# Decode products on GpSimd, whole-head state runs, paired readout transposes and earlier loads for a mean

## The chip, the core and the metric

The kernel runs on one core of a Trainium2 chip. The core has a matrix engine (TensorE, in the profile PE, with its weight loads as PEld), a vector engine (VectorE, DVE), a scalar engine (ScalarE, ACT), a general engine (GpSimd, POOL) and a queue processor (SyncE, SP) that issues most transfers between the chip's memory and the on-chip buffers. Matrix products land in banks of a small accumulator memory (PSUM), and another engine must read them out before a bank can be used again. The metric is the device time of one execution in microseconds; the time before is the median of 3 runs.

## What is computed

One inference step of a two-layer decoder, at once for a prompt of 1024 tokens and for 8 decode sequences with one new token each. The first layer mixes tokens by gated linear attention with 4 heads (key width 96, value width 192), in parallel with attention into 256 memory tokens; the second by windowed attention. Each layer ends in an MLP with a squared ReLU, and every part has a norm before and after it. The part of the decode step that matters here is, for each sequence b and head h,

```
S_new[b,h] = exp(g[b,h])[:, None] * S[b,h] + k[b,h][:, None] * v[b,h][None, :]     # 96 x 192
o[b,h]     = q[b,h] @ S_new[b,h]                                                   # 192
```

`S_new` is an output, and `o` goes, normed and multiplied with a gate silu(r), into the output projection `w_out` of the layer together with the 1024 prompt tokens.

## The kernel before, in words

All activations are kept transposed, features on the 128 partitions and tokens along the free axis, in three chunks of 384, 384 and 264 columns; the last one has the 8 decode columns at its end. Products in 32-bit precision are built of three passes (high x high, high x low, low x high), so a 128 x 384 output tile of a projection with 1024 inputs is 8 x 3 = 24 matrix steps. A float tile is split into its high part by a cast on ScalarE (L158) and its low part by a subtraction on VectorE (L159).

The order of the work on each engine is made by a planner: each instruction has a priority, by its place in the code unless `high_priority` lifts it, and the planner takes for each engine the first one that its cost model holds to be ready. The order is then fixed, and at run time each engine works through its list in order and waits where it must. Transfers on SP go in order too. Buffers come from rings (`bufs=2` means two).

The stage of the change is the end of the first layer's mixer. `r_units` (from L1525) computes the gate for row tiles 3, 4, 5 of each chunk: nine units, chunk by chunk, each one projection and a chain of elementwise steps (L1542 to L1549) whose result goes to a scratch tensor `srd` (L1550). The loop over the nine units (L2001) steps the decode generator `gla_dec` after every second unit. For each head h that generator loads the state `sin` (96 partitions, 8 sequences x 192; L1951) and the values `vb`, broadcast to all 96 partitions from a scratch tensor `vdd` (L1953), and then, for each of the 8 sequences, ScalarE scales the state (L1957) and VectorE adds key times value to it (L1958). The state is stored (L1959). `readout` multiplies queries and states (L1965), 8 products of 32 rows, and copies the result (L1967); the readout of a head is issued when the next head has been, and that of the last head at the end, before the norm of the heads.

`make_o0` makes the input of the output projection for one chunk, in six row tiles: it loads the gate from `srd` (L1985, two buffers), transposes up to three blocks of tokens on TensorE into a bank (L1988, two banks; L1990 for the decode columns of the last chunk), multiplies bank and gate on VectorE (L1992) and splits the result. Chunk 0 is made after the sixth gate unit. `out_proj` then runs eight output tiles per chunk (`part`); chunk 1 is made after three output tiles of chunk 0 and chunk 2 after three more.

In `mlp` the up-projection runs over pairs of output tiles, seven products each in the order `ORDER`; `product` ends in `evict` (L722 for the first product, L724 to L736). `square_mean` loads a chunk of the residual in four parts (L813, two buffers), squares them on ScalarE (L187), adds the squares on VectorE (L194) and forms their mean on TensorE. It is called for pairs 2, 3 and 4 at the fourth product (L998).

Of the kernel before, what the change touches and what calls it, by code (L numbers as in the profile page):

```python
# [8 lines left out]
F32 = mybir.dt.float32  # L9
# [7 lines left out]
P = 128  # L17
D = 1024
KT = 8
# [30 lines left out]
def hybrid_decoder_step(ctx: ExitStack, tc: tile.TileContext, A, O):  # L50
# [31 lines left out]
    srd = dram.tile([P, 6, NT], F32, tag="srd", name="srd")  # L82
    mkd = dram.tile([2, P, 2, MEM], F32, tag="mkd", name="mkd")
    wfd = dram.tile([12, P, KT, P], F32, tag="wfd", name="wfd")
    vdd = dram.tile([NDEC, 768], F32, tag="vdd", name="vdd")
    mvd = dram.tile([2, P, 2, MEM], F32, tag="mvd", name="mvd")
    apd = dram.tile([2, P, NPL, 2, HALF], F32, tag="apd", name="apd")
    awd = dram.tile([2, 7, NJ, P, 2, HALF], F32, tag="awd", name="awd")
# [545 lines left out]
                h = 2 * hp + j  # L634
                nc.vector.tensor_copy(by_group(dq[rows, hp, :]), otv[rows, hp, :, h : h + 5 : 4])

    def out_proj(l, make_o, src_pool, st, ff, xsrc, psum=True, oh0=None):
        wO = st.enter_context(tc.tile_pool(name=nm("wO"), bufs=5, reuse_waits="tile"))
        f0 = ff.pools[0]
        if psum:  # L640
            set_extra(st.enter_context(tc.tile_pool(name=nm("pmo"), bufs=2, space=PSUM, reuse_waits="tile")), 2)
        W = [wload(wA if m < 3 else wO, A["w_out"][l, m]) for m in range(KT)]
        OH, FT = {}, {}

        def prep(c):
            if c == 0 and oh0:
                OH[c] = oh0
                return
            OH[c] = xtiles(c)
            make_o(c, OH[c])  # L650

        R = {}

        def part(c, ms, pool):
            n = CH[c][1]
            if c not in FT:
                FT[c] = pool.tile([P, KT, n], F32, tag="f", name=nm("f"))
                R[c] = Residual(c, FT[c], G_MIXPOST + l, xsrc[c], G_FFNPRE + l)
            for m in ms:
                ps = mmps()  # L660
                proj(ps, W[m], OH[c], n)
                with first():
                    nc.scalar.copy(FT[c][:, m, :], ps[:, :n])
                R[c].feed(m)

        prep(0)
        part(0, range(0, 3), f0)
        prep(1)
        part(0, range(3, 6), f0)
        prep(2)  # L670
        part(0, range(6, 8), f0)
        src_pool.close()
        f2 = ff.open("right")
        f1 = ff.open("rest")
        xsp[0] = ff.rest.enter_context(tc.tile_pool(name=nm("xs"), bufs=2, side="right", reuse_waits="tile"))
        unit = 3 * KT * 384
        res = [R[0].finish(1.3 * unit)]
        part(1, range(KT), f1)
        res.append(R[1].finish(1.3 * unit))
        part(2, range(KT), f2)  # L680
        res.append(R[2].finish(1.3 * unit))
        set_extra(None, 0)
        ff.f = [FT[c] for c in range(3)]
        return res
# [74 lines left out]
    def mlp(l, X, ff):  # L759
# [48 lines left out]
        def square_mean(c):  # L808
            c0, n = CH[c]
            st = Stats(n, "sx")  # L810
            for j in range(4):
                xs = tmp3([P, 2, n])
                nc.sync.dma_start(xs, xd[c][:, 2 * j : 2 * j + 2, :])  # L813
                st.add(xs)
            v = st.mean(X[c][1], 8 * 3 * 4 * SUB)
            nc.scalar.activation(X[c][1], v, AF.Square, scale=math.sqrt(EPS * D / P))

        K1, K2 = slice(0, 4), slice(4, 8)
        pieces = [
# [159 lines left out]
        for t, (j, i) in enumerate(items):  # L979
            if i == ORDER[0]:  # L980
                if j == 0:
                    tiles = [tp.tile([P, 768], F32, tag=tag, name=nm("c")) for tag in ("t3", "t3", "tq", "tq")]
                    rows = [x[:, :HALF] for x in tiles]
                else:
                    tiles = [ff.pools[j % 2].tile([P, 4, HALF], F32, tag="f", name=nm("aw"))]
                    rows = [tiles[0][:, q] for q in range(4)]
            if xsteps:
                next(xsteps.pop(0))
                if xsteps:
                    next(xsteps.pop(0))  # L990
            prepare(t + (3 if j == 0 else 5))
            product(j, i, rows)
            if i == ORDER[0] and pend is not None:
                factors(*pend[2:])
                store(*pend)
                pend = None
            if i == ORDER[3] and 2 <= j < 5:
                square_mean(j - 2)  # L998
            if i == ORDER[-1]:
                more = w4.tile([P, 3, HALF], F32, tag="w4", name=nm("am"))  # L1000
                pend = (j, tiles, rows, more)
# [382 lines left out]
    with ExitStack() as sl0:  # L1384
# [10 lines left out]
        with ExitStack() as sla:  # L1395
# [349 lines left out]
            with ExitStack() as sg:  # L1745
# [139 lines left out]

                def after_first():
                    pend()
                    nc.sync.dma_start(vdd[:, :384], vrow)
                gp = sg.enter_context(tc.tile_pool(name="glb", bufs=2, reuse_waits="tile"))
                S = gp.tile([DK, H, DV], F32, tag="S", name="S", bufs=1)  # L1890

# [38 lines left out]
                for i in range(NB):  # L1930
                    if i == 4:
                        pend()
                        nc.sync.dma_start(vdd[:, 384:], vrow)
                    gla_block(1, i)
                in_r([2])
                nc.sync.dma_start(O["sg_prompt"].rearrange("h k v -> k h v"), S)
# [7 lines left out]
        def gla_dec(dp, d1):  # L1944
            qmk = d1.tile([DK, H, NDEC, 32], F32, tag="qmk", name="qmk")
            nc.gpsimd.memset(qmk, 0.0)
            last = None
            for h in range(H):
                hv = slice(h * DV, h * DV + DV)
                sin = dp.tile([DK, NDEC, DV], F32, tag="sin", name=nm("sin"))  # L1950
                nc.sync.dma_start(sin, A["state_gla"][:, h].rearrange("b k v -> k b v"))  # L1951
                vb = dp.tile([DK, NDEC, DV], F32, tag="vb", name=nm("vb"))
                nc.sync.dma_start(vb, vdd[:, hv].unsqueeze(0).to_broadcast([DK, NDEC, DV]))  # L1953
                for e in range(2):
                    nc.vector.tensor_copy(qmk[:, h, e::2, e], qd[:DK, QIDX[h], e::2])
                for bb in range(NDEC):
                    nc.scalar.mul(sin[:, bb, :], sin[:, bb, :], eg[:, h * NDEC + bb : h * NDEC + bb + 1])  # L1957
                    STT(sin[:, bb, :], vb[:, bb, :], qd[:DK, KIDX[h], bb : bb + 1], sin[:, bb, :], ALU.mult, ALU.add)  # L1958
                nc.sync.dma_start(O["sg_sample"][:, h].rearrange("b k v -> k b v"), sin)  # L1959
                def readout(h=h, hv=hv, sin=sin):  # L1960
                    ops = stps()
                    row = Row()
                    for e in range(2):
                        for g in range(4):
                            row(nc.tensor.matmul(ops[32 * g : 32 * g + 32, :DV], qmk[:, h, 2 * g + e, :],  # L1965
                                                 sin[:, 2 * g + e, :], start=(e == 0), stop=(e == 1)))
                    nc.vector.tensor_copy(vdec[:, hv], ops[:, :DV])  # L1967

                if last:
                    last()  # L1970
                last = readout
                yield
            last()
            head_norm(vdec, [vdec[:, h * DV : h * DV + DV] for h in range(H)], P, d1)

        ff = Sums()
        with ExitStack() as so:
            srp = so.enter_context(tc.tile_pool(name="srp", bufs=2, reuse_waits="tile"))

            def make_o0(c, ohl):  # L1980
                c0, n = CH[c]
                oh, ol = ohl
                for m in range(6):
# [7 lines left out]
                                         ident.rearrange("p (g c) -> p g c", c=32)[:, :, :2], start=True, stop=True)  # L1991
                    TT(sr, tps[:, :n], sr, ALU.mult)  # L1992
                    split(oh[:, m, :], ol[:, m, :], sr)
                split(oh[:, 6:8, :], ol[:, 6:8, :], qm[:, :, c0 : c0 + n])

            with ExitStack() as sd:
                dp = sd.enter_context(tc.tile_pool(name="gdec", bufs=2, side="right", reuse_waits="tile"))
                d1 = sd.enter_context(tc.tile_pool(name="gdec1", bufs=1, side="right", reuse_waits="tile"))
                gt = sd.enter_context(tc.tile_pool(name="gt", bufs=2, reuse_waits="tile"))
                dec = gla_dec(dp, d1)  # L2000
                for u, _ in enumerate(r_units([3, 4, 5], pool=gt)):  # L2001
                    if u % 2 == 0:
                        next(dec, None)
                    if u == 5:
                        oh0 = xtiles(0)
                        make_o0(0, oh0)
            X = out_proj(0, make_o0, svp, so, ff, [A[f"xT{c}"] for c in range(3)], False, oh0)
        pmd.close()

# [477 lines left out]
def _arrays(inp):  # L2487
# [46 lines left out]
    wg[:, 1:17] = inp["w_gate_up"][0]  # L2534
    wg[0, 0] = inp["b_gate"][0]
    a["wg"] = wg.reshape(GR, 2, 192)
    a["state_gla"] = np.ascontiguousarray(inp["state_gla"][0])
    mk = inp["cache_mem_k"].reshape(2, NDEC, MEM, 2, P)
    a["mem_kT"] = np.ascontiguousarray(mk.transpose(0, 1, 4, 3, 2))
    a["mem_v"] = np.ascontiguousarray(  # L2540
# [28 lines left out]
def hp_list(hp):  # L2569
# [2 lines left out]


_OUT = {
    "yT": (P, KT, NT), "sg_prompt": (H, DK, DV), "sg_sample": (NDEC, H, DK, DV),
    "swa_kp": (P, 2, WIN), "swa_vp": (P, 2, WIN), "swa_ks": (NDEC, WIN, 256), "swa_vs": (NDEC, WIN, 256),
    "mem_k": (2, P, 2, MEM), "mem_v": (2, P, 2, MEM),
}
# [2 lines left out]
def _unpack(o):  # L2581
# [3 lines left out]
    sp = [np.ascontiguousarray(o[k].transpose(2, 1, 0)).reshape(1, WIN, 4, 64) for k in ("swa_kp", "swa_vp")]  # L2585
    return (
        np.ascontiguousarray(y[:SEQ])[None], np.ascontiguousarray(y[SEQ:])[:, None],
        o["sg_prompt"][None, None], o["sg_sample"][None], sp[0], sp[1],
        o["swa_ks"].reshape(NDEC, WIN, 4, 64), o["swa_vs"].reshape(NDEC, WIN, 4, 64), mem[0], mem[1],
    )  # L2590

# [16 lines left out]
```

## Time and profile before

| what | value |
|---|---|
| median of 3 runs | 2121.37 us (2118.39 to 2122.22) |
| the profiled execution: time / span | 2120.73 us / 2118.9 us |
| TensorE busy | 2098.3 us, 99% |
| VectorE busy | 1537.3 us, 73% |
| ScalarE busy | 1104.3 us, 52% |
| GpSimd busy | 116.6 us, 6% |
| granted TensorE clock | 1.0 |

The span runs from the first to the last instruction of the profiled execution. An engine's time is busy while it executes an instruction; matrix steps overlap, so that a step's own duration (0.33 us for 128x384) is longer than the distance to the next one. A row of a timeline gives start, duration, engine, line, operation, output<-inputs and shapes, and in brackets how long the engine stood idle before and which instruction ended that. A row of waits gives who waited for whom, us in total, how often, and the longest.

### The profile page before, as it was taken

The numbers are of one execution on the slowest core, as the hardware profiler recorded it, in microseconds if no ns is written. First come the engines' busy times: TensorE is split into PE (matmuls) and PEld (weight loads), VectorE is DVE, ScalarE is ACT, GpSimd is POOL, SyncE is SP. The second block draws the span as 40 slices with busy tenths as digits, with TensorE's granted clock in tenths as the row PEclk, the third lists the DMA queues.
The fourth block names the chain that finished last, engine by engine and source line by source line (L and its number), as shares of the span: only waits on it lengthen the run. The fifth ranks groups of instructions, "written<-read, shape, count | busy, mean of one in ns | idle before, by whom it ended". The sixth has DMA issues, their size and how long they took to land.

```text
span 2118.9 us, 41850 instructions
## 1 busy us (share of the span) xinstructions
PE 2098.3 (99%) x16870; PEld 2026.3 (96%) x16870; DVE 1537.3 (73%) x2869; ACT 1104.3 (52%) x2211; POOL 116.6 (6%) x176
## 2 busy tenths in 40 slices
PE   8999999999999999999999999999999999999998
PEld 6979999899999999999999988899999999999998
DVE  7657648669887777855788457677987777865767
ACT  6365536457645444333555256676664454433454
POOL 0012000000000000034200002000000000000010
PEclk9999999999999999999999999999999999999999
DMA  5521117443654459667444304425454437935345
GB/s 174 168 85 43 41 51 193 151 143 121 193 166 131 145 165 318 224 221 250 161 126 137 104 22 142 158 96 175 140 189 162 163 115 257 314 103 170 101 130 151
DMA packets 143768, 323.22 MB, mean 153 GB/s; under 512 B 16153, under 2 KB 58321, under 8 KB 143217
## 3 DMA queue, kind: packets, MB, share of 16 engines
q1 hardware_dynamic: 125712, 275.20, 40.5%
q0 software_dynamic: 8816, 32.47, 4.6%
q10 hardware_dynamic: 9040, 12.82, 1.6%
q8 instruction: 134, 2.20, 0.4%
q14 instruction: 66, 0.54, 0.1%
HBM read 227.78 MB, written 93.74 MB: 152 GB/s over the span
## 4 chain that ended last, share of the span: by engine, by line
PE 90%; DVE 5%; DMA 3%; ACT 2%; issue 1%; SPq 0%; DVEq 0%; ACTq 0%
PE mm L268 10%; PE mm L280 7%; PE mx L268 7%; PE mx L903 6%; PE mx L905 5%; PE mx L904 5%; PE mx L1148 5%; PE mx L1149 5%; PE mx L1150 5%; PE mm L903 3%; PE mm L905 3%; PE mm L904 3%; PE mm L1148 2%; PE mm L1149 2%; PE mm L1150 2%; PE kv L268 2%
## 5 line engine op out<-in xcount | busy, mean ns | idle before, releaser
L158 ACT CAST wh<-ws 128x512 fp32r<-128x512 f32 (+1 forms) x271 | 199.5, 737 | 302.1 <-PE mx L904 96.8
L903 PE MATMUL mx<-xf,wh 128*128 128x258 f32 x1048 | 297.2, 284 | 0.8 <-DVE aw L732 0.8
L905 PE MATMUL mx<-xf,wl 128*128 128x258 f32 x1048 | 295.7, 282 | 0.0
L904 PE MATMUL mx<-xf,wh 128*128 128x258 f32 x1048 | 295.5, 282 | 0.0
L159 DVE TENSOR_TENSOR wl<-ws,wh 128x512 fp32r<-128x512 f32 (+1 forms) x271 | 226.0, 835 | 54.5 <-ACT wh L158 48.5
L158 ACT CAST wh<-wr 128x1024 fp32r<-128x1024 f32 x102 | 106.9, 1048 | 280.8 <-PE sx L1149 265.3
L1148 PE MATMUL mx<-sa,wh 128*128 128x258 f32 x840 | 237.4, 283 | 0.0
L1149 PE MATMUL mx<-sa,wh 128*128 128x258 f32 x840 | 235.9, 281 | 0.0
L1150 PE MATMUL mx<-sa,wl 128*128 128x258 f32 x840 | 235.9, 281 | 0.0
L159 DVE TENSOR_TENSOR wl<-wr,wh 128x1024 fp32r<-128x1024 f32 x102 | 126.2, 1237 | 139.7 <-ACT wh L158 139.2
L903 PEld LDWEIGHTS mx<-xf,wh 128*128 128x128 f32 x1048 | 197.6, 189 | 1.6 <-ACT aw L943 1.0
L904 PEld LDWEIGHTS mx<-xf,wh 128*128 128x128 f32 x1048 | 198.0, 189 | 0.4
L905 PEld LDWEIGHTS mx<-xf,wl 128*128 128x128 f32 x1048 | 197.8, 189 | 0.0
L1148 PEld LDWEIGHTS mx<-sa,wh 128*128 128x128 f32 x840 | 159.0, 189 | 0.1
L1149 PEld LDWEIGHTS mx<-sa,wh 128*128 128x128 f32 x840 | 158.7, 189 | 0.1
L1150 PEld LDWEIGHTS mx<-sa,wl 128*128 128x128 f32 x840 | 158.3, 188 | 0.0
L268 PE MATMUL mm<-xh,wh 128*128 128x384 f32 (+1 forms) x480 | 155.2, 323 | 0.0
L159 DVE TENSOR_TENSOR sa<-ra,sa 128x1032 fp32r<-128x1032 f32 (+1 forms) x128 | 140.7, 1099 | 20.0 <-ACT sa L158 19.6
L268 PE MATMUL mm<-xh,wl 128*128 128x384 f32 (+1 forms) x480 | 152.4, 317 | 0.0
L268 PE MATMUL mm<-xl,wh 128*128 128x384 f32 (+1 forms) x480 | 152.3, 317 | 0.0
L158 ACT CAST sa<-ra 128x1032 fp32r<-128x1032 f32 (+1 forms) x128 | 120.9, 945 | 52.2 <-PE sf L1150 23.5
L903 PE MATMUL mm<-xf,wh 128*128 128x258 f32 x520 | 147.3, 283 | 0.0
(602 smaller groups left out, 6194.2 us busy)
## 6 DMA issues: line engine op xcount, KB each, us to landing
ra<-awd SPq DMA_DIRECT2D x92, 516.0 KB, 4.4
ws<-in_w_up SPq DMA_DIRECT2D x64, 512.0 KB, 6.3
wr<-in_w_downb SPq DMA_DIRECT2D x64, 512.0 KB, 6.0
awd<-aw SPq DMA_DIRECT2D x26, 1032.0 KB, 7.6
awd<-am SPq DMA_DIRECT2D x28, 774.0 KB, 8.5
ws<-in_w_out SPq DMA_DIRECT2D x26, 512.0 KB, 3.8
ws<-in_w_in_a SPq DMA_DIRECT2D x20, 512.0 KB, 3.8
ws<-wfd SPq DMA_DIRECT2D x15, 512.0 KB, 3.8
```

The lines of the kernel that those rows point to most:

```text
L158: nc.scalar.copy(hi, src)
L159: (eng or nc.vector).tensor_tensor(lo, src, f32(hi), ALU.subtract)
L268: mm = nc.tensor.matmul(ps[:M, :n], w_[:, k, :M], x_[:, k, :], start=(i == 0), stop=(i == 3 * KT - 1))
L280: nc.tensor.matmul(ps[:, :n], w_[:, k, :], x_[:, k, :], start=(k == 0 and t == 0), stop=(k == KT - 1 and t == 2))
L903: nc.tensor.matmul(ps, wh(k), xh, start=(k == 0), stop=False)
L904: nc.tensor.matmul(ps, wh(k), xl, start=False, stop=False)
L905: mm = nc.tensor.matmul(ps, wl(k), xh, start=False, stop=(k == n - 1))
L1148: nc.tensor.matmul(ps, wh[:, q, ms], h, start=(jj == 0 and q == 0), stop=False)
L1149: nc.tensor.matmul(ps, wh[:, q, ms], lo, start=False, stop=False)
L1150: mm = nc.tensor.matmul(ps, wl[:, q, ms], h, start=False, stop=end)
```

## The change

Three places are edited.

In `gla_dec`, GpSimd multiplies keys and values of all eight sequences of a head in one operation, in place in `vb`; ScalarE scales the state as before, and VectorE adds the products four sequences at a time. The state input and output and the scratch tensor `vdd` get a layout with the head outermost and the sequences inside a partition's row, so that each partition's part of a head is one run of 8 x 192 numbers; the host lays the state out that way before the launch and back after it.

`make_o0` becomes a generator that stops after every second row tile. Chunk 0's pairs are made after gate units 5, 6 and 7 (counted from 0), chunk 1's after output tiles 1, 2, 3 of chunk 0, chunk 2's after output tiles 4, 5, 6.

`square_mean` becomes a generator: its first two loads stand behind the first product of a pair (`ORDER[0]`) and the rest behind the fourth (`ORDER[3]`), where all of it stood; the square of a part now stands in the code behind the next part's load.

```
-    vdd = dram.tile([NDEC, 768], F32, tag="vdd", name="vdd")
+    vdd = dram.tile([H, NDEC, DV], F32, tag="vdd", name="vdd")
...
-        prep(0)
-        part(0, range(0, 3), f0)
-        prep(1)
-        part(0, range(3, 6), f0)
-        prep(2)
-        part(0, range(6, 8), f0)
+        for m in range(KT):
+            part(0, [m], f0)
+            if m == 1:
+                made = prep(1)
+            if m == 4:
+                made = prep(2)
+            if 1 <= m < 7:
+                next(made)
...
             st = Stats(n, "sx")
+            got = []
             for j in range(4):
                 xs = tmp3([P, 2, n])
                 nc.sync.dma_start(xs, xd[c][:, 2 * j : 2 * j + 2, :])
-                st.add(xs)
+                got.append(xs)
+                if j == 1:
+                    yield
+                if j:
+                    st.add(got[j - 1])
+            st.add(got[3])
             v = st.mean(X[c][1], 8 * 3 * 4 * SUB)
             nc.scalar.activation(X[c][1], v, AF.Square, scale=math.sqrt(EPS * D / P))
+            yield
...
+            if i == ORDER[0] and 2 <= j < 5:
+                means = square_mean(j - 2)
+                next(means)
             if i == ORDER[3] and 2 <= j < 5:
-                square_mean(j - 2)
+                next(means)
...
-                nc.sync.dma_start(sin, A["state_gla"][:, h].rearrange("b k v -> k b v"))
+                nc.sync.dma_start(sin, A["state_gla"][h])
                 vb = dp.tile([DK, NDEC, DV], F32, tag="vb", name=nm("vb"))
-                nc.sync.dma_start(vb, vdd[:, hv].unsqueeze(0).to_broadcast([DK, NDEC, DV]))
+                nc.sync.dma_start(vb, vdd[h].unsqueeze(0).to_broadcast([DK, NDEC, DV]))
                 for e in range(2):
                     nc.vector.tensor_copy(qmk[:, h, e::2, e], qd[:DK, QIDX[h], e::2])
+                nc.gpsimd.tensor_tensor(vb, vb, qd[:DK, KIDX[h], :].unsqueeze(2).to_broadcast([DK, NDEC, DV]), ALU.mult)
                 for bb in range(NDEC):
                     nc.scalar.mul(sin[:, bb, :], sin[:, bb, :], eg[:, h * NDEC + bb : h * NDEC + bb + 1])
-                    STT(sin[:, bb, :], vb[:, bb, :], qd[:DK, KIDX[h], bb : bb + 1], sin[:, bb, :], ALU.mult, ALU.add)
-                nc.sync.dma_start(O["sg_sample"][:, h].rearrange("b k v -> k b v"), sin)
+                    if bb % 4 == 3:
+                        TT(sin[:, bb - 3 : bb + 1, :], sin[:, bb - 3 : bb + 1, :], vb[:, bb - 3 : bb + 1, :], ALU.add)
+                nc.sync.dma_start(O["sg_sample"][h], sin)
...
                     split(oh[:, m, :], ol[:, m, :], sr)
-                split(oh[:, 6:8, :], ol[:, 6:8, :], qm[:, :, c0 : c0 + n])
+                    if m == 5:
+                        split(oh[:, 6:8, :], ol[:, 6:8, :], qm[:, :, c0 : c0 + n])
+                    if m % 2:
+                        yield
...
-                    if u == 5:
+                    if u == 4:
                         oh0 = xtiles(0)
-                        make_o0(0, oh0)
+                        made = make_o0(0, oh0)
+                    if u > 4:
+                        next(made, None)
```

The two stores of the decode values into `vdd` and the host's handling of the state follow the new layout.

More of the change, by code (lines that the diff above doesn't have):

```diff
@@ L635, in mem_dec_steps, with out_proj @@
                 nc.vector.tensor_copy(by_group(dq[rows, hp, :]), otv[rows, hp, :, h : h + 5 : 4])
-    def out_proj(l, make_o, src_pool, st, ff, xsrc, psum=True, oh0=None):
+    def out_proj(l, make_o, src_pool, st, ff, xsrc, psum, oh0):
         wO = st.enter_context(tc.tile_pool(name=nm("wO"), bufs=5, reuse_waits="tile"))
@@ L643, in out_proj @@
         OH, FT = {}, {}
+        OH[0] = oh0
         def prep(c):
-            if c == 0 and oh0:
-                OH[c] = oh0
-                return
             OH[c] = xtiles(c)
-            make_o(c, OH[c])
+            return make_o(c, OH[c])
         R = {}
@@ L1887, in after_first @@
                     pend()
-                    nc.sync.dma_start(vdd[:, :384], vrow)
+                    nc.sync.dma_start(vdd[:2].rearrange("h b v -> b h v"), vrow.rearrange("b (h v) -> b h v", h=2))
                 gp = sg.enter_context(tc.tile_pool(name="glb", bufs=2, reuse_waits="tile"))
@@ L1932, in hybrid_decoder_step @@
                         pend()
-                        nc.sync.dma_start(vdd[:, 384:], vrow)
+                        nc.sync.dma_start(vdd[2:].rearrange("h b v -> b h v"), vrow.rearrange("b (h v) -> b h v", h=2))
                     gla_block(1, i)
@@ L2536, in _arrays @@
     a["wg"] = wg.reshape(GR, 2, 192)
-    a["state_gla"] = np.ascontiguousarray(inp["state_gla"][0])
+    a["state_gla"] = np.ascontiguousarray(inp["state_gla"][0].transpose(1, 2, 0, 3))
     mk = inp["cache_mem_k"].reshape(2, NDEC, MEM, 2, P)
@@ L2574 @@
 _OUT = {
-    "yT": (P, KT, NT), "sg_prompt": (H, DK, DV), "sg_sample": (NDEC, H, DK, DV),
+    "yT": (P, KT, NT), "sg_prompt": (H, DK, DV), "sg_sample": (H, DK, NDEC, DV),
     "swa_kp": (P, 2, WIN), "swa_vp": (P, 2, WIN), "swa_ks": (NDEC, WIN, 256), "swa_vs": (NDEC, WIN, 256),
@@ L2587, in _unpack @@
         np.ascontiguousarray(y[:SEQ])[None], np.ascontiguousarray(y[SEQ:])[:, None],
-        o["sg_prompt"][None, None], o["sg_sample"][None], sp[0], sp[1],
+        o["sg_prompt"][None, None], np.ascontiguousarray(o["sg_sample"].transpose(2, 0, 1, 3))[None], sp[0], sp[1],
         o["swa_ks"].reshape(NDEC, WIN, 4, 64), o["swa_vs"].reshape(NDEC, WIN, 4, 64), mem[0], mem[1],
```

## The prediction

> **What bounds the kernel now.** I read the page's first part first, then the waits of TensorE over the whole span.
>
> ```profile
> span 2118.9 us, 41850 instructions
> PE 2098.3 (99%) x16870; PEld 2026.3 (96%) x16870; DVE 1537.3 (73%) x2869; ACT 1104.3 (52%) x2211; POOL 116.6 (6%) x176
> ```
>
> TensorE is busy for 2098.3 of 2118.9 us. The change takes no matrix work away and adds none, so all that it can win is time in which TensorE waits, or switches clumsily between kinds of work, and there are only 20.6 us of plain idleness in the whole program. The next view (waits of TensorE; line, releaser, us in total, times, longest) says which of these belong to the touched lines.
>
> ```profile
> PE ot L1988 <- DVE sr L1992: 2.4, 3, 1.2
> ...
> PE mx L903 <- DVE aw L732: 0.8, 1, 0.8
> ```
>
> Two are in reach: the readout transposes of L1988, 2.4 us, which wait until VectorE has emptied their bank (L1992), and 0.8 us in the second layer's up-projection. The rows left out lie at the start, in the second layer's projections and at the end. The timeline of TensorE places the first:
>
> ```profile
> 362.38 0.55 PE L1988 MATMUL ot<-ident,vtok 128*128 128x128 f32 x3 [0.92 <-DVE sr L1992]
> 388.58 1.01 PE L1988 MATMUL ot<-ident,vtok 128*128 128x128 f32 x6 [0.32 <-DVE sr L1992]
> 398.18 0.55 PE L1988 MATMUL ot<-ident,vtok 128*128 128x128 f32 x3 [1.15 <-DVE sr L1992]
> ```
>
> The edited stage therefore lies at 322 to 416 us. How full VectorE is there (stretch: length, then busy time of PE, PEld, DVE, ACT, POOL with counts, clock, DMA share, GB/s):
>
> ```profile
> 356.00:380.00 24.00, 23.05 (x171) 20.05 (x170) 22.49 (x53) 17.64 (x41) 0.00 (x0) 1.00 0.78 215
> ```
>
> From 356 to 380 us VectorE is busy for 22.5 of 24 us and TensorE loses 0.95; GpSimd does nothing there. The granted clock is 1.00 throughout.
>
> **The change part by part.** *Decode products.* The rows of the state tile (min/median/max ns) and of a load's landing:
>
> ```profile
> L1957 ACT ACTIVATE sin<-sin,eg x32: 438/442/457, 331.3 to 367.2; 96x192 f32<-96x192 f32 x32
> L1958 DVE SCALAR_TENSOR_TENSOR sin<-vb,qd,sin x32: 404/410/416, 336.2 to 378.6; 96x192 f32<-96x192 f32 x32
> DMA to landing us min/median/max: 3.9/5.6/7.2
> L194 DVE TENSOR_TENSOR tq<-tq,tq x85: 411/703/960, 9.8 to 2088.4; 128x768 f32<-128x768 f32 x39, 128x528 f32<-128x528 f32 x15, 128x516 f32<-128x516 f32 x13, 128x264 f32<-128x264 f32 x12
> L257 POOL TENSOR_TENSOR t<-t,gains x24: 1032/1052/1937, 892.9 to 1020.8; 128x512 f32<-128x512 f32 x24
> L1810 POOL TENSOR_TENSOR qk<-qk,tq x8: 1265/1282/1557, 179.5 to 213.9; 96x512 f32<-96x512 f32 x8
> ```
>
> Removed: 32 x 0.410 = 13.1 us of VectorE. Added: 8 additions of 96x768; the nearest row is the 128x768 addition, up to 0.96, so 8 x 0.96 = 7.7 us. VectorE is relieved of 5.4 us. ScalarE keeps its 32 scalings. GpSimd gets four products of 96x1536. One operand is broadcast, as in L257, so 3 x 1.05 = 3.2 us each; by L1810, with two whole tensors, 3 x 1.28 = 3.8. I take 3.2. GpSimd has no other work in the stage, but each product must wait for its values' broadcast and then delays the first addition; head by head that is covered, as a head's readout is issued one head later, except the last head, whose readout follows its own additions.
>
> Does the product cost VectorE anything? Two views, of VectorE and GpSimd, show one meeting:
>
> ```profile
> 895.34 1.63 DVE L159 TENSOR_TENSOR wl<-wr,wh 128x1024 fp32r<-128x1024 f32 x1 [0.53 <-ACT wh L158]
> 901.04 1.23 DVE L159 TENSOR_TENSOR wl<-wr,wh 128x1024 fp32r<-128x1024 f32 x1 [2.93 <-ACT wh L158]
> 894.82 1.05 POOL L257 TENSOR_TENSOR t<-t,gains 128x512 f32<-128x512 f32 x1
> ```
>
> The product ran to 895.87, and the subtraction that began at 895.34 took 1.63 instead of 1.23 us: 0.40 of the 0.53 us of overlap were added to it. So a product can hold up VectorE for nearly its own length, 4 x 3.2 = 12.6 us at most, and the relief of 5.4 turns into a burden of 7.2. At least it costs nothing, where VectorE is busy with an operation on PSUM or waits. I take it that the two cancel: VectorE as late as now, 0 on TensorE; bounds below, with the rivals.
>
> The Trainium skill, "SBUF — State Buffer", section "SBUF: two separate sides", says why: VectorE and GpSimd share a port pair that is "an exclusive lock, not a bandwidth split", and a VectorE operation with two SBUF inputs fully waits for a GpSimd operation that reads SBUF. The subtraction above agrees. By that rule alone the relief would be a loss of up to 7.2 us of VectorE time, which is the slower rival below.
>
> *The last head's readout.* Today its matrix products go out in pieces, as the 410 ns steps trickle in (timeline of TensorE):
>
> ```profile
> 344.18 0.34 PE L268 MATMUL mm<-xh,wl 128*128 128x384 f32 x1
> 344.45 0.86 PE L1965 MATMUL sf<-sin,qmk 96*32 96x192 f32 x16
> 345.24 0.44 PE L268 MATMUL mm<-xh,wh 128*128 128x384 f32 x1
> 345.52 0.34 PE L268 MATMUL mm<-xl,wh 128*128 128x384 f32 x1
> 345.69 0.34 PE L268 MATMUL mm<-xh,wl 128*128 128x384 f32 x1
> ...
> 377.15 0.34 PE L268 MATMUL mm<-xh,wh 128*128 128x384 f32 x1
> 377.41 0.51 PE L1965 MATMUL sx<-sin,qmk 96*32 96x192 f32 x2
> 377.86 0.45 PE L268 MATMUL mm<-xl,wh 128*128 128x384 f32 x1
> 378.14 0.34 PE L268 MATMUL mm<-xh,wl 128*128 128x384 f32 x1
> ...
> 379.62 0.84 PE L1965 MATMUL sx<-sin,qmk 96*32 96x192 f32 x10
> ```
>
> Projections follow each other at 0.17 (345.52 to 345.69). A whole head (x16) stretches 344.18 to 345.52, 1.34, which is 1.0 beyond two steps of 0.17. A piece of x2 stretches 377.15 to 378.14, 0.99, so 0.65 beyond. The last head goes in four pieces, three of x2 and one of x10: 3 x 0.65 + about 1.0 = 2.95 against 1.0. With two additions, of batches 0 to 3 and 4 to 7, it can fall into two pieces at most, as the readout takes batches 0, 2, 4, 6, 1, 3, 5, 7: 0.65 + 1.0. Gain 1.3 us; bounds 0 (the order stays) and 2.0 (one piece).
>
> *Readout transposes.* Row tiles are made two at a time: chunk 0's after the gate units 5, 6, 7 instead of all after 5; chunk 1's after output tiles 1, 2, 3 instead of after 2; chunk 2's after 4, 5, 6 instead of after 5. Two row tiles fill the two banks, and a unit of 24 steps between the pairs, 24 x 0.17 = 4.2 us, less in the short chunk, gives VectorE time to empty them. That speaks for all three waits to go, 2.4 us. Against it stands the ring of two row tiles; rows of L1985, and what its loads wait for on SP's queue:
>
> ```profile
> DMA to landing us min/median/max: 2.1/2.7/5.3
> SPq L1985 <- DVE xl L159: 10.7, 8, 2.5
> L1992 DVE TENSOR_TENSOR sr<-ot,sr x18: 425/547/558, 361.8 to 421.4; 128x384 f32<-128x384 f32 x12, 128x264 f32<-128x264 f32 x6
> 369.20 0.92 ACT L158 CAST xh<-sr 128x384 fp32r<-128x384 f32 x2
> 391.38 1.02 DVE L159 TENSOR_TENSOR xl<-sr,xh 128x384 fp32r<-128x384 f32 x2
> ```
>
> A pair takes landing 2.7 to 5.3, multiplication 2 x 0.55, casts 0.92 and subtractions 1.02, thus 5.7 to 8.3 us, while the pairs are asked for every 4.2 (24 steps) and somewhat more for the transposes between. The stall of 1.15 at 398.18 is of this kind and the change does not touch the ring. I take half, 1.2; bounds: all 2.4, and a loss (rival two).
>
> Pairs also mean fewer switches: the single row tiles at 362.38 and 398.18 and others like them become pairs. The first step after a piece takes 0.28 instead of 0.17 (345.24 to 345.52), so I put a switch at 0.1; six fewer are 0.6, of which I take 0.5, and the bounds are 0 and 1.0.
>
> *State in whole-head runs.* Both state transfers and the broadcast keep their bytes (590 KB) but move 6 KB at once instead of 768 B. The 16 DMA engines were 78% busy from 356 to 380; landing, 5.6, will fall. Only ScalarE's scaling waits for it, no TensorE row does: 0. Stores and loads keep their number and their order on SP; two broadcast-source stores become finer, 768 B runs, off the path.
>
> *Loads for a mean.* SP's queue, and ScalarE and TensorE behind it, in the second layer:
>
> ```profile
> 1529.81 0.43 SPq L959 DMA_DIRECT2D awd<-am  x1
> 1530.32 11.20 SPq L813 DMA_DIRECT2D t<-xd  x4
> 1538.55 0.85 ACT L187 ACTIVATE tq<-t 128x768 f32<-128x768 f32 x1 [6.46 <-DMA t<-xd]
> 1541.12 0.36 PE L903 MATMUL mx<-xf,wh 128*128 128x258 f32 x1 [0.82 <-DVE aw L732]
> 1549.09 0.35 ACT L722 COPY aw<-mx 128x258 f32<-128x258 f32 x1
> ```
>
> ScalarE waits 6.46 for the first load, VectorE's sum waits behind it, and TensorE loses 0.82. In the code the loads belong to product 5 of pair 2, but they are out at 1530, ahead of that pair's first result (L722 at 1549): the planner already pulls them up to where their buffers come free. A place three products earlier in the code is still later than that. I take 0; bounds 0 and the 0.8.
>
> **Sum.** 1.3 + 1.2 + 0.5 + 0 + 0 = 3.0 us off the profiled execution, 2120.73 (span 2118.9 and 1.8 around it): 2117.7. That execution is 0.6 below the median of the runs, 2121.37, so against the median I say 2118.4.
>
> **The rivals.** *One: everything lands.* 2.0 + 2.4 + 1.0 + 0.8 = 6.2: 2115.2. For it: VectorE is nearly full where the waits are, and gets relief; against it: the 1.15 us belong to the ring and the load is already out.
>
> *Two: the ring takes the gain back.* Rigid pairs every 4.2 us and more against a loop of 5.7 to 8.3: after the slack of the banks, the last two pairs or so wait 1 to 2 us each. The 2.4 stay, in other places, and a little more; the 1.3 and 0.5 remain at best: 2119.5 to 2122, no change.
>
> *Three, slower: the products hold VectorE.* Place: heads 2 and 3, whose products fall among the first row tiles at 356 to 380. VectorE works in order, so the multiplication that frees a bank stands behind a held subtraction, and the next transposes, and all of TensorE, behind it. Price: two products of 3.2 = 6.4, plus the old 2.4 staying, less 1.8 from the readout and switches: +4.6, 2126.0. It decides once a product starts within a product's length before such a multiplication. For it: 22.49 of 24 us; against: the four additions left in that stretch cost 3.8 against 16 x 0.41 = 6.6 us of steps.
>
> **How the numbers follow.** Forecast 0.45 (its own range 2116.5 to 2120), rival one 0.20, two 0.20, three 0.15. A measurement of this kernel tells about 0.2%, 4.2 us, from no change: below 2117.1 or above 2125.6. Faster: rival one and a fifth of the forecast, 0.29. Slower: most of rival three, 0.13. The rest, 0.58, is no change that can be told. The range 2115 to 2124.5 leaves out the ends of rivals one and three.
>
> **What would show it.** Right: L1958's 32 steps gone, 8 additions near 0.95, four products near 3.2 us on GpSimd; L1965's last head in at most two pieces; the waits of L1988 between 0.5 and 2 us; the first L813 load of the second layer still some 20 us before pair 2's first result, and TensorE's 0.8 us there. Wrong: L1992 late behind a VectorE operation lengthened beside a product; L1988 waiting over 3 us; waits of TensorE in stages that the diff does not name.

## The result, and the profile after

| | before | after |
|---|---|---|
| median of 7 runs each, side by side | 2120.5 us (2118.39 to 2123.69) | 2127.16 us (2125.99 to 2130.26) |
| ratio after to before | | 1.0034, 95% interval 1.0025 to 1.0043 |
| profiled execution: time / span | 2120.73 / 2118.9 us | 2128.43 / 2126.6 us |

The changed kernel is about 7 us slower. The forecast was 2118.4 us with a range up to 2124.5; of the forecasts made, the slower rival, at 2126.0, is the nearest. Ratios and intervals in this document are of fast runs; one run of 4912.57 us, among the twelve of the mean alone, was slow and stands in that kernel's median but not in its ratio.

The page's first part, of the kernel after:

```profile
span 2126.6 us, 41846 instructions
PE 2099.5 (99%) x16870; PEld 2027.5 (95%) x16870; DVE 1543.6 (73%) x2845; ACT 1106.3 (52%) x2211; POOL 129.8 (6%) x180
```

VectorE has 24 instructions fewer, as intended (32 steps gone, 8 additions new), and yet 6.3 us more busy time. The edited rows themselves, first the additions and then the products, are what the diff promises (min/median/max ns):

```profile
L1971 DVE TENSOR_TENSOR sin<-sin,vb x8: 941/944/951, 338.8 to 377.2; 96x768 f32<-96x768 f32 x8
L1967 POOL TENSOR_TENSOR vb<-vb,qd x4: 2747/2872/3005, 333.6 to 361.4; 96x1536 f32<-96x1536 f32 x4
```

Part of the additional VectorE time sits beside the products. The timelines of GpSimd and then of VectorE, after, for the four products:

```profile
333.58 2.75 POOL L1967 TENSOR_TENSOR vb<-vb,qd 96x1536 f32<-96x1536 f32 x1 [8.88 <-ACT sin L1969]
343.45 2.75 POOL L1967 TENSOR_TENSOR vb<-vb,qd 96x1536 f32<-96x1536 f32 x1 [7.12 <-DMA vb<-vdd]
349.71 3.00 POOL L1967 TENSOR_TENSOR vb<-vb,qd 96x1536 f32<-96x1536 f32 x1 [3.52 <-DMA vb<-vdd]
361.39 3.00 POOL L1967 TENSOR_TENSOR vb<-vb,qd 96x1536 f32<-96x1536 f32 x1 [8.67 <-DMA vb<-vdd]
```

```profile
334.30 3.11 DVE L159 TENSOR_TENSOR wl<-ws,wh 128x1024 fp32r<-128x1024 f32 x1 [2.73 <-ACT wh L158]
343.58 3.03 DVE L1558 SCALAR_TENSOR_TENSOR t<-t,y 128x384 f32<-128x384 f32 x1
350.03 3.10 DVE L1559 SCALAR_TENSOR_TENSOR t<-t,y 128x384 f32<-128x384 f32 x1
361.81 2.99 DVE L1559 SCALAR_TENSOR_TENSOR t<-t,y 128x384 f32<-128x384 f32 x1
365.52 0.94 DVE L1971 TENSOR_TENSOR sin<-sin,vb 96x768 f32<-96x768 f32 x1
...
370.27 0.56 DVE L1558 SCALAR_TENSOR_TENSOR t<-t,y 128x384 f32<-128x384 f32 x1 [0.81 <-ACT y L1557]
...
371.02 0.55 DVE L1559 SCALAR_TENSOR_TENSOR t<-t,y 128x384 f32<-128x384 f32 x1
```

Every product meets one VectorE operation that takes about 3 us. Away from a product the same operations take 0.56 and 0.55 us (the last two rows) and, for the 128x1024 subtraction, 1.21 to 1.23. Taking the normal durations off, 1.9 + 2.5 + 2.5 + 2.4 = 9.3 us are added, and each of these operations ends 0.4 to 1.1 us after its product does. Less the relief (32 x 0.410 - 8 x 0.944 = 5.6) this is 3.7 of the 6.3 us; the rest can't be told from what differs between kernels without a product, which are up to 2.9 us above the kernel before. The Trainium skill, "SBUF — State Buffer", section "Who interferes with whom", has this as a rule: a VectorE instruction with two SBUF inputs contends with a GpSimd instruction that reads SBUF, and the later one fully waits. All four rows agree.

What TensorE loses by it (waits of TensorE between 330 and 416 us, after; before, this view had one row, the 2.4 us of the readout transposes):

```profile
PE sf L1978 <- DVE sin L1971: 3.9, 2, 3.1
PE ot L2001 <- DVE sr L2005: 1.9, 3, 0.9
PE mx L268 <- ACT wh L158: 1.7, 1, 1.7
PE sx L1978 <- DVE sin L1971: 0.8, 1, 0.8
PE mm L268 <- DVE wl L159: 0.5, 1, 0.5
```

The sum is 8.8 us, 6.4 more than before. Largest is the readout of the third head, which waits for its additions. There is a second loss behind it (timeline of TensorE, after):

```profile
366.52 0.52 PE L1978 MATMUL sf<-sin,qmk 96*32 96x192 f32 x4 [3.07 <-DVE sin L1971]
367.85 0.94 PE L1978 MATMUL sf<-sin,qmk 96*32 96x192 f32 x12 [0.81 <-DVE sin L1971]
368.73 1.69 PE L2001 MATMUL ot<-ident,vtok 128*128 128x128 f32 x6
...
370.66 0.42 PE L268 MATMUL mm<-xh,wl 128*128 128x264 f32 x1
370.88 0.42 PE L268 MATMUL mm<-xh,wh 128*128 128x264 f32 x1
...
372.07 0.28 PE L268 MATMUL mm<-xh,wh 128*128 128x264 f32 x1
372.19 0.28 PE L268 MATMUL mm<-xl,wh 128*128 128x264 f32 x1
```

The steps at 370 us follow each other at 0.22 us and those at 372 at 0.12. The clock fits (stretches of the kernel after; the third number from the end is the granted clock):

```profile
366.00:368.00 2.00, 0.67 (x8) 0.29 (x12) 2.00 (x5) 0.00 (x0) 0.00 (x0) 1.00 0.27 98
368.00:370.00 2.00, 2.00 (x17) 1.23 (x12) 1.46 (x4) 1.90 (x5) 0.00 (x0) 0.62 0.71 187
370.00:372.00 2.00, 2.00 (x11) 2.00 (x11) 1.73 (x5) 2.00 (x6) 0.00 (x0) 0.53 0.29 108
372.00:374.00 2.00, 2.00 (x18) 2.00 (x18) 2.00 (x5) 2.00 (x5) 0.00 (x0) 1.00 0.38 103
```

After its wait TensorE ran at about half clock for some 3.4 us: (1 - 0.62) x 2 + (1 - 0.53) x 2 = 1.7 us of work lost. Together 6.4 + 1.7 = 8.1 us, against 7.7 between the two profiled executions; the rest of the program adds up to little.

### The profile page after: what moved, and what is told of

Read it like the earlier page. It is cut to its first block, busy times and chain, and to the rows that moved or that the text cites. A ratio compares the mean times of both kernels' runs of the same rounds, so it can differ in the third digit from the quotient of the medians.

```text
span 2126.6 us, 41846 instructions
## 1 busy us (share of the span) xinstructions
PE 2099.5 (99%) x16870; PEld 2027.5 (95%) x16870; DVE 1543.6 (73%) x2845; ACT 1106.3 (52%) x2211; POOL 129.8 (6%) x180
## 4 chain that ended last, share of the span: by engine, by line
PE 86%; DVE 7%; DMA 3%; ACT 3%; issue 1%; SPq 0%; DVEq 0%; ACTq 0%
PE mm L268 8%; PE mm L280 7%; PE mx L911 6%; PE mx L913 5%; PE mx L912 5%; PE mx L1159 5%; PE mx L1160 5%; PE mx L1161 5%; PE mx L268 5%; PE mm L911 3%; PE mm L913 3%; PE mm L912 3%; PE mm L1159 2%; PE mm L1160 2%; PE mm L1161 2%; PE kv L268 2%
```

## The experiments

Three theories were written down before the first runs. H: the GpSimd product holds VectorE, and this is the loss. R: the new places of the row tiles cost. L: the additions come late because a product stands ahead of them at all, on whatever engine. The ratios are against the kernel before, run beside each; its medians were 2119.8 to 2120.7 us. One caution holds for all: the planner arranges an edited kernel anew, so that a difference of 1 or 2 us may come from the order of unedited work.

**The product alone.** The kernel before, with the product on GpSimd and the eight additions, and nothing else of the change.

```
+                nc.gpsimd.tensor_tensor(vb, vb, qd[...KIDX[h], :]...to_broadcast([DK, NDEC, DV]), ALU.mult)
-                    STT(sin[:, bb, :], vb[:, bb, :], qd[...], sin[:, bb, :], ALU.mult, ALU.add)
+                    if bb % 4 == 3:
+                        TT(sin[four], sin[four], vb[four], ALU.add)
```

> The kernel before with one edit: the four products on GpSimd and the eight additions; state layout, row tiles and mean loads as before. Theory H (a product of 2.75 us holds VectorE's two-input operations for nearly its whole length, four times): four VectorE operations of about 3 us that take 0.5 to 1.2 otherwise, TensorE waits of 2 to 5 us for the state in the decode readout, 2125 to 2129 us. Theory R (the new places of the row tiles cost the time): 2118 to 2121 us, waits of the transposes as before.

Measured: 2127.68 us, ratio 1.0031 (1.0019 to 1.0043), as H had it; the wait is longer than H had it and at another place. One part of the change makes the whole loss. The wait and a held operation (waits of TensorE, then VectorE's timeline):

```profile
PE ot L1990 <- DVE sr L1994: 7.5, 2, 7.1
```

```profile
363.27 2.83 DVE L1549 SCALAR_TENSOR_TENSOR t<-t,nglan 128x384 f32<-128x384 f32 x1
366.03 0.94 DVE L1960 TENSOR_TENSOR sin<-sin,vb 96x768 f32<-96x768 f32 x1
...
368.50 0.54 DVE L1994 TENSOR_TENSOR sr<-ot,sr 128x384 f32<-128x384 f32 x1
```

Here the victim is the one that rival three named: the multiplication that frees a bank (L1994, the prediction's L1992) stands behind the held operation and the additions, and the next transposes wait 7.1 us in one go. That is far more than any one hold (363.27 is 2.2 us longer than usual): VectorE brings the lateness of three earlier holds with it. R, by which this kernel should have stayed near the one before, falls for the main part.

**All but the product.** The changed kernel with the 32 steps of before in place of product and additions.

```
-                nc.gpsimd.tensor_tensor(vb, vb, qd[...], ALU.mult)
-                    if bb % 4 == 3:
-                        TT(sin[four], sin[four], vb[four], ALU.add)
+                    STT(sin[:, bb, :], vb[:, bb, :], qd[...], sin[:, bb, :], ALU.mult, ALU.add)
```

> The changed kernel with the 32 multiply-add steps on VectorE back and no product on GpSimd; layout, paired row tiles and mean loads stay. Theory H: no VectorE operation over 1.3 us in the stage, no wait for the state above 1 us, 2116 to 2121 us. Theory R: 2125 to 2128 us, as the changed kernel.

Measured: 2117.86 us, ratio 0.9988 (0.9979 to 0.9997), 2.5 us faster than the kernel before and the fastest of these kernels. No VectorE operation of the stage takes over 1.3 us, as H had it. The transposes wait 0.3 us in all. What is left, against the expectation of no wait for the state above 1 us, is the last head's last piece (timeline of TensorE, then stretches, of this kernel):

```profile
373.96 0.51 PE L1976 MATMUL sx<-sin,qmk 96*32 96x192 f32 x2 [1.89 <-DVE sin L1969]
```

```profile
374.00:376.00 2.00, 2.00 (x9) 1.70 (x10) 2.00 (x5) 0.00 (x0) 0.00 (x0) 0.84 0.93 293
376.00:378.00 2.00, 2.00 (x8) 2.00 (x8) 2.00 (x6) 1.87 (x6) 0.00 (x0) 0.50 0.81 219
378.00:380.00 2.00, 2.00 (x13) 1.89 (x12) 2.00 (x6) 1.43 (x6) 0.00 (x0) 0.81 1.01 360
```

A wait of 1.89 us is followed by the same stretch of half clock, (0.16 + 0.50 + 0.19) x 2 = 1.7 us.

**The product on VectorE, and on ScalarE.** The changed kernel with the product moved off GpSimd, once as one VectorE operation, once as eight ScalarE scalings per head.

```
-                nc.gpsimd.tensor_tensor(vb, vb, qd[...], ALU.mult)
+                nc.vector.tensor_tensor(vb, vb, qd[...], ALU.mult)
```

```
-                nc.gpsimd.tensor_tensor(vb, vb, qd[...], ALU.mult)
+                    nc.scalar.mul(vb[:, bb, :], vb[:, bb, :], qd[:DK, KIDX[h], bb : bb + 1])
```

> The changed kernel with the product of a head on VectorE instead of GpSimd, else the same. It adds 4 x 1.7 = 7 us of VectorE work where the holds added about 4 x 2.5 = 10. Theory H: the only long operations are the products themselves; 2119 to 2125 us, below the changed kernel. Theory L (the additions come late because a separate product stands before them, whoever makes it): 2126 to 2129 us.

> The changed kernel with the products on ScalarE, 8 steps of about 0.44 per head, 3.5 us, so that they are as long as on GpSimd but hold nobody. Theory H: no VectorE operation over 1.3 us, 2118 to 2122 us. Theory L: the product is as late as on GpSimd, 2125 to 2129 us.

Measured: 2121.25 us, ratio 1.0004 (0.9995 to 1.0013), and 2119.95 us, ratio 0.9996 (0.9987 to 1.0005). A product of 1.75 us on VectorE itself, four times, costs less than one of 2.75 to 3.0 us beside it on GpSimd. In both kernels the additions stand behind a product, so L falls for the main part. Against the kernel without the product (2117.86) they are 3.4 and 2.1 us slower, where the product on GpSimd costs 9.3; what share of the small remainder is L's is not shown.

**The product in eighths.** The changed kernel, with the product as eight GpSimd operations of one sequence each, whose factor is one number per partition.

```
+                for bb in range(NDEC):
+                    nc.gpsimd.tensor_scalar(vb[:, bb, :], vb[:, bb, :], qd[:DK, KIDX[h], bb : bb + 1], None, ALU.mult)
```

> The changed kernel with each head's product on GpSimd in eight steps of 96x192, each with a per-partition factor, instead of one of 96x1536. Theory H, by length: VectorE can run between the steps and a hold lasts one step, a few tenths of a us; no VectorE operation of its kind over twice its usual time; 2118 to 2123 us. If it is the total of GpSimd's time that counts and not the length of one product: 2125 to 2129 us, as the changed kernel.

Measured: 2124.37 us, ratio 1.0017 (1.0008 to 1.0026), a miss for H, which had it lower, and for the rival, which had it higher. The group of these operations:

```profile
L1968 POOL TENSOR_SCALAR vb<-vb,qd 96x192 f32<-96x192 f32 x32 | 33.9, 1074 | 11.6 <-DMA vb<-vdd 9.2 <-DVE t L1559 2.3
```

The long holds are gone (no addition over 1.18 us), but an eighth takes 1.07 us where the whole takes 2.75 to 3.0, so a head's product now takes 8 x 1.07 = 8.6 us and the additions are late for another reason. VectorE alone waited 4.9 us for these products between 330 and 380 us, so the time of this run does not price the holds.

**The pairs alone, and the mean alone.** The kernel before with the readout in pairs of row tiles only, and with the earlier loads of `square_mean` only.

```
+                    if m % 2:
+                        yield
...
+                    if u == 4:
+                        made = make_o0(0, oh0)
+                    if u > 4:
+                        next(made, None)
```

```
+            if i == ORDER[0] and 2 <= j < 5:
+                means = square_mean(j - 2)
+                next(means)
```

> The kernel before with the new places of the row tiles alone. If the prediction's term for them is right: waits of the transposes below 1.5 us in total instead of 2.4, 2117 to 2120 us. Rival two (the ring of two row tiles takes it back): waits of 2.4 us and more, 2120 to 2123 us.

> The kernel before with the earlier place of the loads for the mean alone. If the planner had already pulled them up: the first load of the second layer again right behind the store of the three sums, 2119 to 2122 us. If the place matters: the load some 9 us earlier against the products, and TensorE's 0.8 us there gone, 2117 to 2120 us.

Measured: 2119.17 us, ratio 0.9996 (0.9987 to 1.0005), and 2120.96 us, ratio 1.0003 (0.9995 to 1.0012); neither differs from before by what can be told. In the pairs' kernel the transposes' wait fell from 2.4 to 0.5 us, but the last head's piece began to wait (waits of TensorE):

```profile
PE sx L1966 <- DVE sin L1959: 1.3, 1, 1.3
...
PE ot L1989 <- DVE sr L1993: 0.5, 2, 0.3
```

The granted clock from 356 to 380 us is 0.93 in this kernel (1.00 before), so behind the 1.3 us another (1 - 0.93) x 24 = 1.7 us go: together more than the transposes gave. With the mean's kernel the loads go out where they went before, right behind the store of the sums (SP's queue, below). TensorE's 0.8 us wait there is absent all the same; in the changed kernel, where the loads stand at the same place in the code, it is 1.0, so it does not follow that place:

```profile
1527.98 0.43 SPq L966 DMA_DIRECT2D awd<-am  x1
1528.50 15.27 SPq L814 DMA_DIRECT2D t<-xd  x6
```

**Idle products.** The kernel before, whole, with GpSimd products added whose result nobody reads: the steps stay on VectorE, and no instruction waits for a product's result (only the next load into the values' buffer waits until the product has read it).

```
+                for d in range(0, NDEC, 2):
+                    nc.gpsimd.tensor_tensor(scr, vb[:, d : d + 2, :], qd[..., d : d + 2]..., ALU.mult)
```

> The kernel before, with its 32 multiply-add steps, and beside them on GpSimd the products of each head once more, in four steps of 96x384 into a tile that nobody reads: GpSimd's reading of the on-chip memory without any change in what VectorE must do. Theory H: VectorE operations with two inputs lengthened by up to 0.8 us, some ten of them; 2121 to 2126 us, slower than before. If only the place of the additions behind a product costs: 2119 to 2121.5 us.

Measured: 2127.07 us, ratio 1.0032 (1.0021 to 1.0043), above the 2121 to 2126 that H had. This settles H against L: the same loss with no result awaited. The group of the steps between 330 and 380 us and the wait:

```profile
L1961 DVE SCALAR_TENSOR_TENSOR sin<-vb,qd,sin 96x192 f32<-96x192 f32 x26 | 12.0, 494 | 0.1
...
L1548 DVE SCALAR_TENSOR_TENSOR t<-t,y 128x384 f32<-128x384 f32 x6 | 4.5, 758 | 0.0
```

```profile
368.35 0.90 PE L1991 MATMUL ot<-ident,vtok 128*128 128x128 f32 x3 [5.70 <-DVE sr L1995]
```

The steps of 410 ns take 494 on the mean, and the transposes wait 5.7 us once. This run also tells how a wait comes of short holds. From 333 us to the first multiplication that frees a bank, VectorE executes the same operations in the same order as in the kernel before. Its start can be read from VectorE's timelines (the kernel before, this one, and then the changed kernel):

```profile
361.78 0.55 DVE L1992 TENSOR_TENSOR sr<-ot,sr 128x384 f32<-128x384 f32 x1
```

```profile
367.75 0.54 DVE L1995 TENSOR_TENSOR sr<-ot,sr 128x384 f32<-128x384 f32 x1
```

```profile
367.99 0.54 DVE L2005 TENSOR_TENSOR sr<-ot,sr 128x384 f32<-128x384 f32 x1
```

No operation ahead of it is longer by more than 0.64 us, but the lengthenings add up to 6.3 us, and the multiplication is 6.0 us late: it is the sum of the holds that TensorE feels here.

**Idle memsets.** The same control with GpSimd just as busy, but reading next to nothing: a one-column copy that waits for the head's values, and ten memsets of the scratch tile.

```
+                nc.gpsimd.tensor_copy(scr[:, 0, :1], vb[:, 0, :1])
+                for d in range(10):
+                    nc.gpsimd.memset(scr, 0.0)
```

> The kernel before, with GpSimd work added that reads next to nothing: once a head's value rows have landed, one GpSimd copy of a 96x1 column of them into a scratch tile, and then ten memsets of that 96x384 tile, about 4.2 us a head by the memsets of the profile (128x256 0.31, 128x512 0.54 us); that is as long as the four 96x384 products of the idle products were (4.1 us a head). Nothing reads the scratch tile; the steps on VectorE stay. Theory H in its strict form (VectorE is held by GpSimd operations that read SBUF): no VectorE operation beside the memsets gets longer (L1548 0.55, L1543 0.35 us as before), TensorE's waits stay those of before, 2119 to 2122 us. Rival G (any GpSimd work at this place does it): holds of 1 us and more and the time of the idle products, 2125 to 2128 us.

Measured: 2120.38 us, ratio 1.0004 (0.9995 to 1.0013). The groups between 330 and 380 us, GpSimd's and VectorE's:

```profile
L1959 POOL MEMSET scr<- 96x384 f32 x40 | 17.2, 429 | 2.3
```

```profile
L1962 DVE SCALAR_TENSOR_TENSOR sin<-vb,qd,sin 96x192 f32<-96x192 f32 x31 | 11.7, 407 | 0.4 <-ACT sin L1961 0.2
...
L1548 DVE SCALAR_TENSOR_TENSOR t<-t,y 128x384 f32<-128x384 f32 x6 | 3.3, 547 | 0.0
```

GpSimd is busy for 17.2 us here, for 16.3 with the idle products, and no group of VectorE's operations is longer on the mean than before by more than 0.02 us. GpSimd's work as such does not hold, so rival G falls. A memset is shorter than an idle product (0.43 against 1.02 us) and another operation, so that it is the reading that holds is not isolated. The rule of the Trainium skill, "SBUF — State Buffer", section "Who interferes with whom", that a GpSimd instruction which only writes does not contend with such VectorE instructions, agrees.

**The state sooner.** The changed kernel with the load of the next head's state written one step earlier in the code.

```
+                if h + 1 < H:
+                    ahead = state(h + 1)
                 yield
```

> The changed kernel with one move: the load of the next head's state is sent at the end of a head's step, so that on the sync engine's queue it stands ahead of the next units' gate rows and not behind them. The GpSimd products stay. Theory Q (the hold of product 2 reaches TensorE over the queue: late gate row, its store late, the third head's state load behind it late): the third head's state is sent before 352 us, the wait of TensorE at L1978 for the additions (3.9 us) falls below 1.5 us, 2120 to 2124 us. Rival P (the products' holds late in the stage are enough by themselves, wherever the state load stands): some TensorE wait of 3 us and more stays between 356 and 380, at another line where it is not this one, 2125 to 2128 us.

Measured: 2127.57 us, ratio 1.0041 (1.0028 to 1.0055), and it tells nothing of theories Q and P. The planner left the load where it was, behind a gate row's store (SP's queue):

```profile
354.57 0.34 SPq L1561 DMA_DIRECT2D srd<-t  x1
355.01 0.37 SPq L1962 DMA_DIRECT2D sin<-in_state_gla  x1
```

It counts as a repetition of the change.

## Why the prediction was wrong

**The step that failed** is the one on the product's cost to VectorE: "I take it that the two cancel: VectorE as late as now, 0 on TensorE". The mechanism had been read rightly from one meeting of 0.40 us in the trace of before, and the bounds for VectorE's sum, a relief of 5.4 to a burden of 7.2 us, held: 9.3 us of holds less 5.6 of relief is a burden of 3.7. What was wrong is the middle that was taken. Every one of the four products held an operation for most of its length, 1.9 to 2.5 us, where about 1.4 each would have cancelled the relief. And the sum over the whole stage is not what TensorE sees: by the first multiplication that frees a bank all four holds had come, but only six of the eight additions in place of 24 steps, a relief of 24 x 0.410 - 6 x 0.944 = 4.2 us. VectorE was thus to be about 5 us late there. It was 6.2 us late (367.99 instead of 361.78); the remaining microsecond is not traced. TensorE's waits grew by 6.4 us, and 1.7 went behind them in half clock. The term was put at 0; the product alone measures +7.2 us, and the changed kernel against the one without the product 2127.16 - 2117.86 = +9.3.

The prediction also held the additions' delay to be covered for every head but the last, as a head's readout is issued one head later. The third head's was not covered: its readout waited for its additions, 3.9 us in all.

**Rival three** had the mechanism and, at 2126.0 against 2127.16, nearly the price, but the price is in part luck. It counted two products at 3.2 us, with no relief against them beyond the readout's and the switches' 1.8; measured are four holds, a relief, and the half clock, which it left out. It placed two products at 356 to 380 us; only the fourth began there (361.39), the third at 349.71. Its victim, the multiplication that frees a bank, is that of the product alone and of the idle products; in the changed kernel itself the readout of the third head came to stand first behind the held operation. The condition it named ("once a product starts within a product's length before such a multiplication") was not needed: in the changed kernel the multiplication began 6.6 us after the fourth product had started, in the product alone 6.0, both more than a product's length, as the earlier holds had already made VectorE late. A chance of 0.15 was too little: four products in a stage in which VectorE was busy 22.49 of 24 us could hardly miss an operation with two SBUF inputs, since the gate's chain alone has three such lines per unit.

How the third head came so late can be read from the trace, but no run has isolated it. Three rows, SP's queue after and then before, show it:

```profile
353.95 0.34 SPq L1561 DMA_DIRECT2D srd<-t  x1
354.40 0.37 SPq L1962 DMA_DIRECT2D sin<-in_state_gla  x1
```

```profile
348.67 0.54 SPq L1951 DMA_DIRECT2D sin<-in_state_gla  x1
```

The operation held at 350.03 belongs to a gate row; that row's store left at 353.95, and the third head's load of its state, next in SP's order, at 354.40 instead of 348.67. Part of this is the planner's new order, which put the store ahead of the load. The fourth product then held a later gate row from 361.81, and the head's additions stood behind it.

**The last head's readout** was forecast at two pieces, -1.3 us. It went in two (x4 at 376.88 and x12 at 378.23, with 0.83 us of wait between them), so the form was right; its gain can't be seen beside the loss.

**The readout transposes** were put at waits of 0.5 to 2 us. They measure 1.9 us in the changed kernel, 0.5 with the pairs alone and 0.3 without the product, so there the ring of two row tiles, rival two, did not bind as feared. With the product on ScalarE, though, they wait 4.1 us, the longest 1.73, and one of the multiplications (373.28) stands 0.69 us waiting for its gate's load; the ring's share is not shown. The time did not follow with the pairs alone (-0.8 us by the ratio, not told from 0); in its profile the wait had moved on to the last head and drew half clock after it.

**Whole-head runs** made the state land in 4.3 us on the median instead of 5.6, and nothing on the path shows it: 0, as said. **The mean's loads** did not move, and the mean alone is no change: 0, as said. All parts but the product together were forecast at -3.0 less the readout's share of the additions, thus -1.7; they measure -2.5 us (0.9979 to 0.9997). Which part gave it is not shown: pairs and mean alone can't be told from no change.

## What to carry to other kernels

Before elementwise work is moved to an idle GpSimd, list the VectorE operations with two SBUF inputs that can run beside it, and price each product with a hold of nearly its own length. Add the holds up to the first operation that TensorE waits for, and take off only the relief that comes before it; then follow what stands behind in order (banks, stores, loads on the same queue). A control whose result nobody reads shows in one experiment whether an engine's mere activity costs something. A wait of TensorE of more than a microsecond may cost a slow stretch on top, here 1.7 us of lost work.

## What the runs showed of the hardware

The clock after short waits was not expected. In this stage waits of 1.10 us (product alone, at 399.02), 1.30 (pairs alone), 1.73 (product on ScalarE), 1.82 (state sooner), 1.89 (without the product), 2.12 (eighths), 3.07 (changed kernel) and 3.14 us (state sooner) were each followed by some 3.4 us at about half clock, or 1.7 us of lost work, more than the shortest of these waits themselves. With the 5.70 us of the idle products and the 7.13 us of the product alone the clock stood near half already within the wait and for almost 4 us after it. Not every wait does it: after 1.15 us at 398.18 in the kernel before, 1.36 beside the memsets, 1.55 in the eighths' kernel and 1.69 at 398.43 in the changed kernel the clock stayed at 1.00 (stretch of the changed kernel):

```profile
380.00:416.00 36.00, 31.92 (x187) 29.71 (x186) 26.61 (x53) 20.20 (x39) 0.00 (x0) 1.00 0.56 177
```

Between 1.1 and 1.9 us, then, the length of the wait alone does not tell. The Trainium skill, "TensorE: Matmul & The Clock Gate", Part 1, gives half rate after at least one idle window of about 3.4 us, by a window that runs freely; the length of the slow stretch agrees with it, the idle times of 1.10 to 1.89 us are shorter than such a window.

A GpSimd multiplication of 96x192 by one number per partition took 1.07 us, so that eight of them took three times as long as one operation of 96x1536 with a broadcast operand (2.75 to 3.0). It held VectorE less: no addition or gate operation beside these eighths took more than 0.24 us longer than usual, where the 96x384 products of the idle products, 1.02 us each, made single operations up to 0.64 us longer.

The holding seems to go both ways. In the product-alone kernel the four products took 3.16 to 3.90 us instead of 2.75 to 3.0, and each began while VectorE was in an operation with two SBUF inputs; no run isolates this.

An operation with one input was held too: L1543, a tensor_scalar of 128x384 that takes 0.35 us, took 2.33 beside a product in the product-alone kernel:

```profile
354.05 2.33 DVE L1543 TENSOR_SCALAR t<-t 128x384 f32<-128x384 f32 x1
```

Beside the memsets it did not get longer (0.34 and 0.37 us at 343.88 and 353.04).
